# A long sequence's feed-forward by seven block products for eight (Strassen-Winograd)

## The chip, the cores and the metric

One core of one Trainium2 chip runs one launch: one layer of an encoder over two request groups. The metric is the device time of the launch in microseconds, the median of the runs. The kernel before takes 2230.62 us (three runs, 2229.17 to 2234.43).

A core has the engines PE (matrix products into PSUM, with weight loads that the profile calls PEld), DVE (vector), ACT (scalar functions and copies), POOL (GpSimd), and SP, which here issues nearly all DMAs, in order. Each works through its own list of instructions and waits for the others at semaphores.

## The reference

For each group, n tokens of 1024 features (1024 prompt tokens or 512 sample tokens, each behind 16 meta tokens that are dropped at the end) pass one mixer and one gated feed-forward. What the change touches is the last part:

```python
def conv_glu_sublayer(x, g_ffn, w_ff_gate, w_ff_up, conv_w, conv_b, w_ff_down):
    n = rms_norm(x, g_ffn)
    gate = n @ w_ff_gate
    pad = jnp.pad(gate, ((0, 0), (1, 1), (0, 0)))
    gate = pad[:, :-2] * conv_w[0] + pad[:, 1:-1] * conv_w[1] + pad[:, 2:] * conv_w[2] + conv_b
    return x + (jax.nn.gelu(gate, approximate=False) * (n @ w_ff_up)) @ w_ff_down
    ...
    h = rms_norm(h, g_final)
    return h[:, N_META:]
```

The hidden width is 2816, 22 tiles of 128. The convolution needs gate at the token before and after each one; so the first kept token needs gate of the last meta token, "column 0".

## The kernel before

Activations lie transposed, features on partitions (KT = 8 tiles of 128), tokens along the free axis. All large products are done to nearly F32 accuracy from three reduced ones: `split` (L99) makes of each operand a rounded part (hi, a cast on ACT, L102) and the remainder (lo, a subtraction, L103, on DVE or POOL), and `mm3` (L106) adds hi by hi, hi by lo and lo by hi in PSUM (L108 to L110).

The program works first through the projections and attention of both groups, with the sample group's feed-forward beside the prompt group's attention. Then `mixer_out` of the long (prompt) group, s = 0, adds the output projection to the residual h in chunks of 344, 342 and 340 tokens (`token_chunks`), squares and sums h on ACT and POOL (L486, L487) and makes each chunk's root factor `rstd` with a matmul of ones (L492) and a Newton step (L95, L96). It is merged with the rest of the sample's feed-forward.

Then PSUM is given out anew, eight tiles "mm", and `conv_glu` of s = 0 runs alone to the end of the program:

- It norms h chunk by chunk (L562, DVE) and splits it (L102; L103 on DVE and POOL by turns).
- For each of 11 pairs of tiles it forms gate in three chunks of 342 to 344 columns (two of them halo), 24 matmuls per chunk and tile, with the convolution straight out of PSUM (L585 on ACT, L586 and L588 on DVE). Gelu follows for the pair (L591). Up is formed the same way and multiplied in (L603, DVE), and the product is split.
- The pair's share of the down-projection, 8 output tiles by two chunks of 512 tokens, is formed and added to h in SBUF (L615, DVE).
- In the last pair the down-projection runs in four chunks of 256, and each is normed (L628 ff.) and stored to `yT` while the next runs; the last chunk's sum of squares is done by matmuls of ones (L656).

Weights are loaded by `load_weight` (L121) as 128 x 1024 tiles `w_f` (512 KB, SP, L125), with three buffers, in the order in which they are used, and split on ACT and DVE. Tile pools release a buffer to the next writer when its last reader is done. Nothing but the written order of the code sets the order on each engine in this part.

Of the kernel before, what the change touches and what calls it, by code (L numbers as in the profile page):

```python
# [12 lines left out]
F32 = mybir.dt.float32  # L13
# [7 lines left out]
P = 128  # L21
D = 1024
KT = D // P
NMETA = 16
HD = 64
DFF = 2816
# [57 lines left out]
def pool(ctx, g, name, bufs, side):  # L84
    return ctx.enter_context(g.tc.tile_pool(name=name, bufs=bufs, side=side, reuse_waits="tile"))
# [20 lines left out]
def mm3(g, ps, whi, wlo, xhi, xlo, start, stop):  # L106
    nc = g.nc
    nc.tensor.matmul(ps, lhsT=whi, rhs=xhi, start=start, stop=False)  # L108
    nc.tensor.matmul(ps, lhsT=whi, rhs=xlo, start=False, stop=False)  # L109
    nc.tensor.matmul(ps, lhsT=wlo, rhs=xhi, start=False, stop=stop)  # L110


def dense(g, ps, w, xhi, xlo, c0, cw, order=range(KT)):

    whi, wlo = w
    for i, k in enumerate(order):
        mm3(g, ps, whi[:, k * P:(k + 1) * P], wlo[:, k * P:(k + 1) * P],
            xhi[k][:, c0:c0 + cw], xlo[k][:, c0:c0 + cw], i == 0, i == KT - 1)
# [359 lines left out]
def add_square(g, tp, acc, h, j, c0, cw, eng, bufs=2):  # L478

    nc = g.nc  # L480
    hs = h[:, j, c0:c0 + cw]
    if j == 0:
        nc.scalar.activation(acc, hs, AF.Square)
    else:
        sq = tp.tile([P, cw], F32, name="sq", tag="sq", bufs=bufs)
        nc.scalar.activation(sq, hs, AF.Square)  # L486
        eng.tensor_tensor(out=acc, in0=acc, in1=sq, op=ALU.add)  # L487
# [5 lines left out]
    rsqrt_newton(g, tp, out, ps, cw)  # L493


def mixer_out(g, s, st, side, wp, wb, whole, tag):

    nc, tc = g.nc, g.tc
    C = SEQS[s] + 2
    h, rstd = st.h, st.rstd  # L500
    chunks = token_chunks(s)
    cm = max(w for _, w in chunks)
    with ExitStack() as es:
        mp = pool(es, g, f"fm{s}", 3, side)
        waiting = []

        def finish():
            while waiting:
                c0, cw, acc = waiting.pop(0)
                mean_rsqrt(g, mp, rstd[:, c0:c0 + cw], acc, cw, tag)  # L510

        for group in ([chunks] if whole else [[c] for c in chunks]):
            if whole:
                (xhi, xlo), base = [[x[:, k] for k in range(KT)] for x in st.x], 0
            else:
                xhi = [mp.tile([P, cm], F32R, name="xhi", tag=f"xhi{k}", bufs=2 if k >= K2 else 1) for k in range(KT)]
# [28 lines left out]
            waiting += [(c0, cw, acc[:, c0 - base:c0 - base + cw]) for c0, cw in group]  # L545
        finish()

# [116 lines left out]
        yield 4 * cw  # L664


def merge(a, wa, b, wb):
# [12 lines left out]
def drain(gen):  # L680
    for _ in gen:
        pass
# [4 lines left out]
ML = 2  # L687
K2 = 8
MB = 5
R1, R2, R3 = (1.0, 0.9), (1.0, 0.4), (1.0, 1.0)  # L690


@with_exitstack
def trunk_kernel(ctx, tc, g):
# [5 lines left out]
    for s, N in enumerate(SEQS):  # L700
# [4 lines left out]
        g.vt.append(dram.tile([5, 96, 2 * P], F32, name=f"vt{s}"))  # L705
        g.oT.append(dram.tile([D, N + 1], F32, name=f"oT{s}"))

    nc.scalar.preload_act_table_set(EXP_LN)
    g.vec = const.tile([P, V_N], F32, name="vec")
    nc.sync.dma_start(out=g.vec, in_=g.vec_in)  # L710
# [44 lines left out]
    with ExitStack() as es0:  # L755
# [4 lines left out]
    with ExitStack() as es1:  # L760
        wp = pool(es1, g, "fw1", 2, "left")
        st1 = state(es1, 1, "left", True)

        def sample():
            yield from mixer_out(g, 1, st1, "left", wp, 3, True, "mm")
            yield from conv_glu(es1, g, 1, st1, "left", wp, 3, 1)
        f1 = sample()
        with ExitStack() as es0:
            merge(attention(es0, g, 0, "right"), R2[0], f1, R2[1])
        wp0 = pool(ctx, g, "fw0", 2, "right")  # L770
        st0 = state(ctx, 0, "right", False)
        merge(mixer_out(g, 0, st0, "right", wp0, 3, False, "s"), R3[0], f1, R3[1])
        drain(f1)
    xp = pool(ctx, g, "fx0", 1, "left")
    st0.x = [xp.tile([P, KT, SEQS[0] + 2], F32R, name=nm) for nm in ("xhi", "xlo")]
    g.psum.es.close()
    g.psum = Psum(tc, "psb", mm=8)
    drain(conv_glu(ctx, g, 0, st0, "left", wp0, 3, 2))
    g.psum.es.close()


# [59 lines left out]
```

## Time and profile before

| what | value |
|---|---|
| median of three runs | 2230.62 us (2229.17 to 2234.43) |
| profiled execution | 2230.43 us |
| its span, first to last instruction | 2228.6 us |
| mean granted PE clock | 0.980 |
| long mixer_out's last matmul | starts 1460.29 us |
| first matmul of the long feed-forward | starts 1465.48 us |
| last sum of squares | starts 2216.55 us |

The profile lists, for one execution, the busy time of each engine, the chain of work that ended last, groups of like instructions, DMA issues and, from the trace, single instructions with their start (us from the span's start) and duration. PE's records overlap, since matmuls are pipelined: what one matmul costs is seen from the distance between two starts, not from its duration. A group's row gives the busy time in us, the mean of one in ns, and what ended the idle time of the engine before it.

### The profile page before, as it was taken

To read this page: it belongs to the slowest core of one execution; us is meant where nothing else is said; L and a number is where in the kernel's file an instruction comes from. 1 tells how busy PE (TensorE), PEld (TensorE's weight loads), DVE (VectorE), ACT (ScalarE), POOL (GpSimd) and SP (SyncE) were. 2 spreads that over 40 slices of the span, in tenths; PEclk is the share of its full clock that TensorE was granted. 3 is DMA by queue.
4 is the path that set the end of the run, shared out by engine and by line. 5 is a ranking of instruction groups with operands and counts; after the bars stand their busy time and mean duration, and the time that the engine had idled before them with its cause. 6 is when DMAs were issued, how large, how long until landed. Compare 5 with 4: busy or idle time off the path is not lost.

```text
span 2228.6 us, 36288 instructions
## 1 busy us (share of the span) xinstructions
PE 2128.2 (95%) x13474; PEld 1984.5 (89%) x13474; DVE 1463.7 (66%) x3453; ACT 1069.8 (48%) x1921; POOL 812.3 (36%) x649
## 2 busy tenths in 40 slices
PE   7999998997999999999999999999999999999997
PEld 6888888996987998898988899989999999999997
DVE  6876787767788777788878865784443344433446
ACT  6534566544567566776776655551222221212224
POOL 3465546864445333355444423431111000111005
PEclk9999999998999999999999999999999999999999
DMA  6555335446321322232322125721111111111112
GB/s 226 163 168 191 113 93 157 166 170 196 101 80 54 101 72 65 72 124 80 121 90 76 65 73 172 221 93 48 48 38 57 48 48 48 48 38 57 48 39 76
DMA packets 113137, 219.80 MB, mean 99 GB/s; under 512 B 13728, under 2 KB 69824, under 8 KB 112448
## 3 DMA queue, kind: packets, MB, share of 16 engines
q1 hardware_dynamic: 112960, 217.48, 30.4%
q8 instruction: 106, 1.74, 0.3%
q14 instruction: 71, 0.58, 0.1%
HBM read 168.93 MB, written 48.50 MB: 98 GB/s over the span
## 4 chain that ended last, share of the span: by engine, by line
PE 76%; DVE 12%; issue 4%; ACT 4%; DMA 3%; POOL 2%; SPq 1%; DVEq 0%; ACTq 0%; POOLq 0%
PE ps_mm L108 18%; PE ps_mm L109 18%; PE ps_mm L110 18%; PE ps_t L370 5%; PE ps_s L347 3%; PE ps_s L348 3%; DVE p L349 2%; DVE w_lo L103 2%; PE ps_o L385 1%; PE ps_o L384 1%; PE ps_s L108 1%; PE ps_s L110 1%; PE ps_s L109 1%; DMA w_f<-w_in 1%; DMA x<-xT 1%
## 5 line engine op out<-in xcount | busy, mean ns | idle before, releaser
L108 PE MATMUL ps_mm<-xhi,w_hi 128*128 128x342 f32 (+6 forms) x2320 | 726.5, 314 | 12.4 <-ACT xhi L177 6.4
L109 PE MATMUL ps_mm<-xlo,w_hi 128*128 128x342 f32 (+6 forms) x2320 | 721.3, 311 | 8.8 <-DVE xlo L103 4.6
L110 PE MATMUL ps_mm<-xhi,w_lo 128*128 128x342 f32 (+6 forms) x2320 | 719.8, 310 | 0.0
L108 PEld LDWEIGHTS ps_mm<-xhi,w_hi 128*128 128x128 f32 x2320 | 441.5, 190 | 20.2 <-ACT xhi L177 7.2
L109 PEld LDWEIGHTS ps_mm<-xlo,w_hi 128*128 128x128 f32 x2320 | 441.6, 190 | 16.3 <-DVE xlo L103 6.8
L110 PEld LDWEIGHTS ps_mm<-xhi,w_lo 128*128 128x128 f32 x2320 | 442.1, 191 | 1.0
L102 ACT CAST w_hi<-w_f 128x1024 fp32r<-128x1024 f32 x200 | 207.5, 1047 | 388.9 <-PE ps_mm L109 341.9
L103 POOL TENSOR_TENSOR a_lo<-gate,a_hi 128x256 fp32r<-128x256 f32 (+2 forms) x110 | 120.4, 1097 | 725.6 <-ACT a_hi L102 725.6
L103 DVE TENSOR_TENSOR w_lo<-w_f,w_hi 128x1024 fp32r<-128x1024 f32 x183 | 264.6, 1453 | 125.9 <-ACT w_hi L102 123.8
L349 DVE TENSOR_SCALAR_CACHE_REDUCE p<-ps_s 114x344 f32<-114x344 f32 (+4 forms) x562 | 257.6, 487 | 41.8 <-PE ps_s L348 23.3
L615 DVE TENSOR_TENSOR h<-ps_mm,h 128x512 f32<-128x512 f32 (+1 forms) x288 | 182.0, 644 | 122.3 <-PE ps_mm L110 121.4
L354 ACT ACTIVATE p<-p,nm 114x1040 f32<-114x1040 f32 (+5 forms) x212 | 215.0, 1014 | 87.3 <-DVE nm L352 84.5
L102 ACT CAST pt_hi<-ps_t 128x512 fp32r<-128x512 f32 (+6 forms) x360 | 168.8, 483 | 154.4 <-PE ps_t L370 132.4
L421 POOL TENSOR_TENSOR p<-p,r 128x1040 f32<-128x1040 f32 (+1 forms) x96 | 159.2, 1666 | 188.0 <-DVE r L356 125.7
L109 PE MATMUL ps_mm<-a_lo,w_hi 128*128 128x512 f32 (+1 forms) x576 | 216.1, 375 | 2.1 <-POOL a_lo L103 2.1
L108 PE MATMUL ps_mm<-a_hi,w_hi 128*128 128x512 f32 (+1 forms) x576 | 213.8, 382 | 2.4 <-DVE h L615 1.6
L110 PE MATMUL ps_mm<-a_hi,w_lo 128*128 128x512 f32 (+1 forms) x576 | 215.7, 374 | 0.0
L103 DVE TENSOR_TENSOR pt_lo<-ps_t,pt_hi 128x512 fp32r<-128x512 f32 (+4 forms) x312 | 171.7, 561 | 50.5 <-ACT pt_hi L102 49.0
L347 PE MATMUL ps_s<-k,q 128*114 128x348 f32 (+4 forms) x552 | 184.3, 338 | 14.3 <-DVE p L349 13.7
L370 PE MATMUL ps_t<-ident,p 128*128 128x128 f32 (+7 forms) x1188 | 183.6, 270 | 2.4 <-DVE pt_lo L103 2.1
L348 PE MATMUL ps_s<-k,q 128*114 128x348 f32 (+4 forms) x552 | 172.8, 318 | 1.3 <-DMA q<-qk 1.3
L370 PEld LDWEIGHTS ps_t<-ident,p 128*128 128x128 f32 (+7 forms) x1188 | 140.9, 136 | 31.6 <-issue 6.8
(158 smaller groups left out, 3638.3 us busy)
## 6 DMA issues: line engine op xcount, KB each, us to landing
w_f<-w_gate SPq DMA_DIRECT2D x44, 512.0 KB, 3.5
w_f<-w_up SPq DMA_DIRECT2D x44, 512.0 KB, 3.5
w_f<-w_down SPq DMA_DIRECT2D x44, 512.0 KB, 3.6
w_f<-w_in SPq DMA_DIRECT2D x36, 512.0 KB, 4.1
w_f<-w_out SPq DMA_DIRECT2D x32, 512.0 KB, 3.6
q<-qk SPq DMA_DIRECT2D x32, 257.0 KB, 3.7
q<-qk SPq DMA_DIRECT2D x48, 171.0 KB, 2.9
qk<-hi SPq DMA_DIRECT2D x42, 192.0 KB, 2.0
```

The costliest lines, as they stand in the source:

```text
L102: nc.scalar.copy(hi, src)
L103: (lo_engine or nc.vector).tensor_tensor(out=lo, in0=src, in1=hi.bitcast(F32), op=ALU.subtract)
L108: nc.tensor.matmul(ps, lhsT=whi, rhs=xhi, start=start, stop=False)
L109: nc.tensor.matmul(ps, lhsT=whi, rhs=xlo, start=False, stop=False)
L110: nc.tensor.matmul(ps, lhsT=wlo, rhs=xhi, start=False, stop=stop)
L347: nc.tensor.matmul(ps, lhsT=q[0], rhs=k[:, c0:c0 + cw], start=True, stop=False)
L348: nc.tensor.matmul(ps, lhsT=q[1], rhs=k[:, c0:c0 + cw], start=False, stop=True)
L349: nc.vector.tensor_scalar(out=p[:, c0:c0 + cw], in0=ps, scalar1=HD ** -0.5, scalar2=-3.0e38, op0=ALU.mult, op1=ALU.max, accum_out=mx[:, i: ...
L354: nc.scalar.activation(p, p, AF.Exp, bias=nm, accum_out=l)
L370: nc.tensor.transpose(tps[:, c:c + M], p[:, k0:k0 + kw], g.ident[:M, :M])
L421: nc.gpsimd.tensor_tensor(out=p, in0=p, in1=r.broadcast_to([P, n]), op=ALU.mult)
L615: nc.vector.tensor_tensor(out=hs, in0=ps, in1=hs, op=ALU.add)
```

## The change

The feed-forward of the long sequence is done by blocks of two by two, in the form of Winograd: seven products of blocks for eight, at the price of sums and differences of blocks. A block of the weights is half of a tile's 1024 columns (128 x 512); a block of the inputs is 4 feature tiles by 512 tokens.

**Inputs.** `combine_first` norms x11 and x21 (first 512 tokens) and splits them, within mixer_out's third chunk; it also keeps column 0's input, `x0`. `combine` then norms the other half, in place in h, and makes and splits t1, t2, t3, x22 and t4. Operations alternate between DVE and POOL (L739 differences, L105 remainders). Since h is overwritten, mixer_out stores h to DRAM (`g.h`).

**Gate and up.** For each pair of tiles one call of `winograd` makes gate for both tiles and both token halves, another makes up: 7 products of 12 matmuls with 512 columns. POOL makes the weights' sums s1 to s4. Gate is gathered in SBUF, 1 + 1024 columns for each tile; column 0 comes from 8 matmuls per tile with plain F32 operands of two columns (L824). Convolution, gelu and the product with up now work from SBUF. Seven combined blocks of the pair's activations are stored to DRAM (`g.act`).

**Down.** Outside the pairs' loop, product by product: q = 0 to 5 over 512 columns and q = 6 in two halves of 256, each over 11 pairs with 12 matmuls of 4 output tiles. Weights are loaded as half tiles and stay in SBUF; activations are loaded from `g.act` (L966, four buffers) and split. The residual comes back from `g.h`. The final norm of the second token half runs within q = 6, that of the first half behind its own sums.

```diff
@@ mixer_out
-                w = load_weight(g, wp, g.w_out[j], bufs=wb)
+                w = load_weight(g, wp, g.w_out[j], bufs=wb) if s == 1 else load_halves(g, wp, g.w_out[j])
...
+                    if s == 0:
+                        nc.sync.dma_start(out=g.h[j, :, c0:c0 + cw], in_=h[:, j, c0:c0 + cw])
...
+                elif j > ML and late and group[0] == chunks[-1]:
+                    for _ in range(2):
+                        next(late, None)
...
+def combine(g, st, xp, x):
...
+    def minus(out, a, b, i):
+        (nc.vector if i % 2 else nc.gpsimd).tensor_tensor(out=out, in0=a, in1=b, op=ALU.subtract)
+        return out
...
+    for i in range(HT):
+        normed(g, st, i, 1 + H)
+        kept(g, x, "t1", i, minus(x11[i], x12[i], x11[i], i))
+    for i in range(HT):
+        normed(g, st, HT + i, 1 + H)
+        kept(g, x, "t2", i, minus(x11[i], x22[i], x11[i], i))
+    for i in range(HT):
+        kept(g, x, "t3", i, minus(x12[i], x22[i], x12[i], i))
+    for i in range(HT):
+        kept(g, x, "x22", i, x22[i])
+    for i in range(HT):
+        kept(g, x, "t4", i, minus(x21[i], x21[i], x11[i], i))
...
+def winograd(g, wp, up, x, raw):
...
+    def s_(op, a, b):
+        t = up.tile([P, H], F32, name="w_s", tag="w_s", bufs=SB)
+        nc.gpsimd.tensor_tensor(out=t, in0=a, in1=b, op=op)
+        return t
...
+    s1 = s_(ALU.add, a21, a22)
+    p1 = product(split_half(g, wp, a11), x["x11"])
+    u = tile("u")
+    nc.scalar.copy(u, p1)
+    yield 0, 0, product(split_half(g, wp, a12), x["x21"]), u
+    p5 = product(split_half(g, wp, s1), x["t1"])
+    v = tile("v")
+    nc.scalar.copy(v, p5)
+    s2 = s_(ALU.subtract, s1, a11)
+    p6 = product(split_half(g, wp, s2), x["t2"])
+    add(nc.vector, u, p6, u)
+    add(nc.gpsimd, v, u, v)
+    s3 = s_(ALU.subtract, a11, a21)
+    p7 = product(split_half(g, wp, s3), x["t3"])
+    add(nc.vector, u, p7, u)
+    yield 1, 1, p7, v
+    s4 = s_(ALU.subtract, a12, s2)
+    yield 0, 1, product(split_half(g, wp, s4), x["x22"]), v
+    yield 1, 0, product(split_half(g, wp, a22), x["t4"]), u
...
+                ps = g.psum.tile(P, 2, "mm")
+                for k in range(KT):
+                    nc.tensor.matmul(ps, lhsT=raw[i][:, k * P:(k + 1) * P], rhs=g.x0[:, k],
+                                     start=k == 0, stop=k == KT - 1)
...
+            nc.vector.tensor_tensor(out=t, in0=ps, in1=rest, op=ALU.add)
+            nc.gpsimd.tensor_tensor(out=a, in0=t, in1=a, op=ALU.mult)
...
+        kept_act("x11", x11)
+        kept_act("x21", x21)
+        kept_act("x22", x22)
+        t2 = minus("t2", x22, minus("t1", x12, x11))
+        minus("t3", x22, x12)
+        minus("t4", x21, t2)
...
+    for q, (c0, cw) in [(q, (0, H)) for q in range(6)] + [(6, (0, H // 2)), (6, (H // 2, H // 2))]:
+        ps = [g.psum.tile(P, cw, "mm") for _ in range(HT)]
+        for f in range(NP):
+            w = operand(q, f)
+            if f == 0 and q < 2:
+                a = xs[:, q * H:(q + 1) * H]
+            else:
+                a = op.tile([P, H], F32, name="a_f", tag="a_f", bufs=AF_)[:, :cw]
+                nc.sync.dma_start(out=a, in_=g.act[f, q, :, c0:c0 + cw])
+            ahi, alo = (t[:, :cw] for t in split_act(g, wp, a, cw))
+            w = split_half(g, wp, w)
+            for j in range(HT):
+                mm3(g, ps[j], *block(w, j), ahi, alo, f == 0, f == NP - 1)
```

In the diff, H = 512, HT = 4, the weight halves have five buffers (`w_hi`, `w_lo`), the sums `w_s` two, and `split_half` splits with ACT and DVE. The lines below are what stands on three engines; each row has the line, the operation, its output and inputs and their shape, and xN for N alike in a row. Line numbers are those of the changed kernel where its rows are shown.

On POOL, at the start of the long feed-forward, there stood before only the remainders of the normed chunks (`xlo`) and then those of the first activations (`a_lo`):

```order
L487 TENSOR_TENSOR acc<-acc,sq 128x340
L103 TENSOR_TENSOR xlo<-t,xhi 128x344 x4
L103 TENSOR_TENSOR xlo<-t,xhi 128x342 x4
L103 TENSOR_TENSOR xlo<-t,xhi 128x340 x4
L103 TENSOR_TENSOR a_lo<-gate,a_hi 128x342 x2
```

In the changed kernel, at the same place, the end of the combined inputs (`h` for the differences, `t_lo` and `x_lo` for the remainders; eleven such rows stand ahead) and then the first sums of weights (`w_s`):

```order
L105 TENSOR_TENSOR t_lo<-h,t_hi 128x512
L739 TENSOR_TENSOR h<-h 128x512
L105 TENSOR_TENSOR t_lo<-h,t_hi 128x512 x4
L739 TENSOR_TENSOR h<-h 128x512 x2
L767 TENSOR_TENSOR w_s<-w_f 128x512
L767 TENSOR_TENSOR w_s<-w_s,w_f 128x512
L767 TENSOR_TENSOR w_s<-w_f 128x512
L767 TENSOR_TENSOR w_s<-w_f,w_s 128x512
L767 TENSOR_TENSOR w_s<-w_f 128x512
L780 TENSOR_TENSOR v<-u,v 128x512
```

So s1, which the third product reads, comes behind all of them.

On SP, the queue of the loads, before had whole weight tiles only, in the order of their use:

```order
L125 DMA w_f<-w_down 128x1024 x2
L125 DMA w_f<-w_gate 128x1024 x2
L125 DMA w_f<-w_up 128x1024 x2
L125 DMA w_f<-w_down 128x1024 x2
L644 DMA yT<-y 128x2x256 x16
```

In the changed kernel, from the last store of a difference (`act_101<-a_t`) to the first loads of activations for the down-projection (`a_f`); a name such as a_6 is a half tile of w_down for pair 6:

```order
L850 DMA act_101<-a_t 128x512
L885 DMA a_7_23054<-w_down 128x512
L885 DMA a_8_23078<-w_down 128x512
L885 DMA a_8_23080<-w_down 128x512
L885 DMA a_9_23104<-w_down 128x512
L885 DMA a_10_23128<-w_down 128x512
L885 DMA a_10_23130<-w_down 128x512
L885 DMA a_1_23182<-w_down 128x512
L885 DMA a_1_23184<-w_down 128x512
L885 DMA a_2_23208<-w_down 128x512
L885 DMA a_3_23232<-w_down 128x512
L966 DMA a_f<-act_101 128x512 x4
```

The loads of activations now stand behind a store that waits for POOL, and behind weight loads of later pairs.

On PE, at the first products of gate, the changed kernel has behind the last chunk's sum (`ps_s<-acc,ones_d`) matmuls of 512 columns and among them the two-column ones for column 0 (`x_18861` is `x0`):

```order
L520 MATMUL ps_s<-acc,ones_d 128x340
L110 MATMUL ps_mm<-x_hi,w_hi 128x512 x2
L824 MATMUL ps_mm<-x_18861,w_f 128x2 x8
L111 MATMUL ps_mm<-x_lo,w_hi 128x512
L112 MATMUL ps_mm<-x_hi,w_lo 128x512
L110 MATMUL ps_mm<-x_hi,w_hi 128x512
```

The matmuls of chunks with 344 columns, which stood there before, are gone.

More of the change, by code (lines that the diff above doesn't have):

```diff
@@ L23 @@
 KT = D // P
+H = D // 2
+HT = KT // 2
 NMETA = 16
@@ L113, in dense, with block, split_half, load_whole @@
 def dense(g, ps, w, xhi, xlo, c0, cw, order=range(KT)):
+    for i, k in enumerate(order):
+        mm3(g, ps, *block(w, k), xhi[k][:, c0:c0 + cw], xlo[k][:, c0:c0 + cw], i == 0, i == KT - 1)
+def block(w, k):
     whi, wlo = w
[L116 to L118 removed]
+    if isinstance(whi, list):
+        whi, wlo, k = whi[k // 4], wlo[k // 4], k % 4
+    return whi[:, k * P:(k + 1) * P], wlo[:, k * P:(k + 1) * P]
+def split_half(g, wp, src, lo_engine=None):
+    hi = wp.tile([P, H], F32R, name="w_hi", tag="w_hi", bufs=HB)
+    lo = wp.tile([P, H], F32R, name="w_lo", tag="w_lo", bufs=HB)
+    split(g, hi, lo, src, lo_engine)
+    return hi, lo
+def load_whole(g, wp, src):
+    w = wp.tile([P, D], F32, name="w_f", tag="w_f", bufs=WB)
+    g.nc.sync.dma_start(out=w, in_=src)
+    return w
+def load_halves(g, wp, src):
+    w = load_whole(g, wp, src)
+    parts = [split_half(g, wp, w[:, i * H:(i + 1) * H]) for i in range(2)]
+    return [p[0] for p in parts], [p[1] for p in parts]
 def load_weight(g, wp, src, bufs=2, ahead=2, lo_engine=None):
@@ L664, in conv_glu, with normed, kept, inputs @@
         yield 4 * cw
+def normed(g, st, k, c0):
+    hs = st.h[:, k, c0:c0 + H]
+    g.nc.vector.scalar_tensor_tensor(out=hs, in0=hs, scalar=g.gain[:, V_GFFN + k:V_GFFN + k + 1],
+                                     in1=st.rstd[:, c0:c0 + H], op0=ALU.mult, op1=ALU.mult)
+    return hs
+def kept(g, x, nm, i, src):
+    split(g, x[nm][0][:, i], x[nm][1][:, i], src, g.nc.gpsimd if i % 2 else g.nc.vector)
+def inputs(pl, names):
+    return {nm: [pl.tile([P, HT, H], F32R, name=f"{nm}_{part}") for part in ("hi", "lo")] for nm in names}
@@ new lines, in combine_first @@
+def combine_first(g, st, xp, x):
+    nc = g.nc
+    x.update(inputs(xp, ("x11", "x21")))
+    g.x0 = xp.tile([P, KT, 2], F32, name="x0")
+    for i in range(2):
+        nc.vector.scalar_tensor_tensor(out=g.x0[:, :, i], in0=st.h[:, :, 0], scalar=st.rstd[:, 0:1],
+                                       in1=g.gain[:, V_GFFN:V_GFFN + KT], op0=ALU.mult, op1=ALU.mult)
+    for nm, k0 in (("x11", 0), ("x21", HT)):
+        for i in range(HT):
+            kept(g, x, nm, i, normed(g, st, k0 + i, 1))
+            yield
@@ L689 @@
 MB = 5
+HB = 5
+WB = 3
+SB = 2
+AT = 3
+AF_ = 4
+LAGF = 5
+TS = ("x11", "x21", "t2", "t1", "t3", "x22", "t4")
 R1, R2, R3 = (1.0, 0.9), (1.0, 0.4), (1.0, 1.0)
```

215 lines of the change are left out of this document (199 added, 16 removed).

## The prediction

> **What bounds the kernel now.** First the head of the page and its chain of work, shares of the span by engine.
> ```profile
> span 2228.6 us, 36288 instructions
> PE 2128.2 (95%) x13474; PEld 1984.5 (89%) x13474; DVE 1463.7 (66%) x3453; ACT 1069.8 (48%) x1921; POOL 812.3 (36%) x649
> PE 76%; DVE 12%; issue 4%; ACT 4%; DMA 3%; POOL 2%; SPq 1%; DVEq 0%; ACTq 0%; POOLq 0%
> ```
> The sum below is made against this execution: span 2228.6, time 2230.43, so 1.8 us lie around the span; the median of the runs, 2230.62, is the same within 0.2 us. An average over the program says little about the changed stage, so next the table of windows (us from the start; busy time of PE, PEld, DVE, ACT, POOL; granted clock, DMA share, GB/s).
> ```profile
> 1360.00:1460.00 100.00, 100.00 (x648) 99.50 (x647) 68.08 (x117) 53.58 (x98) 38.65 (x35) 0.99 0.69 214
> 1460.00:1480.00 20.00, 14.96 (x69) 12.35 (x69) 18.27 (x27) 9.62 (x20) 8.46 (x9) 0.83 0.24 82
> 1500.00:1600.00 100.00, 100.00 (x562) 93.22 (x561) 43.24 (x64) 20.91 (x28) 13.97 (x12) 1.00 0.16 52
> 2000.00:2100.00 100.00, 100.00 (x580) 94.93 (x579) 42.87 (x62) 22.11 (x29) 6.86 (x6) 1.00 0.14 48
> ```
> In the long feed-forward (about 1466 to 2217) PE is full, DVE 43%, ACT some 22%, POOL 7 to 14%, DMA 15%. Only PE sets the time there, and the others have room for additions. The one hole is its start, 1460 to 1480. The chain of work by time gives the period of a pair of tiles: the same matmul comes back every 67.14 us.
> ```profile
> 1582.86 0.24 PE ps_mm L108
> 1650.00 0.24 PE ps_mm L108
> 1717.14 0.24 PE ps_mm L108
> ```
>
> **Removed and added on PE.** Overlapping records hide a matmul's cost; the step between the starts of weight loads (PEld), or of matmuls, shows it.
> ```profile
> 1500.01 0.19 PEld L109 LDWEIGHTS ps_mm<-xlo,w_hi 128*128 128x128 f32 x1
> 1502.83 0.19 PEld L109 LDWEIGHTS ps_mm<-xlo,w_hi 128*128 128x128 f32 x1
> 1535.09 0.19 PEld L108 LDWEIGHTS ps_mm<-a_hi,w_hi 128*128 128x128 f32 x1
> 1536.90 0.19 PEld L110 LDWEIGHTS ps_mm<-a_hi,w_lo 128*128 128x128 f32 x1
> 2203.87 0.28 PE L110 MATMUL ps_mm<-a_hi,w_lo 128*128 128x256 f32 x1
> 2205.66 0.28 PE L110 MATMUL ps_mm<-a_hi,w_lo 128*128 128x256 f32 x1
> ```
> Some 342 columns: 18 steps in 2.82 us, 0.157 each. 512 columns: 8 steps in 1.81, 0.226. 256 columns: 15 steps in 1.79, 0.119. Before, a pair has 288 x 0.157 + 96 x 0.226 = 66.9 us, the measured period. After, gate and up have 2 x 84 matmuls of 512 columns: 168 x 0.226 = 38.0.
>
> New beside them are 16 plain F32 matmuls of two columns per pair (line 824 of the change), for gate's column 0. An F32 matmul leaves two records, as the profile's eight calls of L656 show, so 32 records per pair, 352 in all. Nothing like them is in the trace; these rows bound them.
> ```profile
> L656 PEld LDWEIGHTS ps_mm<-sq,ones_d x16: 186/190/192, 2208.1 to 2218.3; 128*128 128x128 f32 x16
> 1332.83 0.57 PEld L370 LDWEIGHTS ps_t<-ident,p 114*128 114x128 f32 x5
> 2216.55 2.32 PE L656 MATMUL ps_mm<-sq,ones_d 128*128 128x256 f32 x10
> ```
> Loads back to back in the second row come (0.57 - 0.19)/4 = 0.095 apart; a whole load alone takes 0.19. I take 0.10, by the row with narrow work that follows itself, and keep 0.19: 3.2 us per pair (to 6.1). Gate and up: 41.2 x 11 = 453 us, of which the first pair's p1, p2 and column 0 (7 us) run before the hole, so 446 to 447 behind it.
>
> Down: q0 to q5 are 6 x 11 x 12 = 792 matmuls, 179.0; q6's two halves 264 x 0.119 = 31.4; the sums of squares are one F32 matmul of 512 columns and, ahead of the last sum, one half's five of 256; by the last row above a record of 256 takes 2.32/10, less its tail 0.215: 4 x 0.215 + 10 x 0.215 = 3. Together 213.5, say 214.
>
> **The start.** These rows show the sum for the last chunk, its rstd, and DVE and POOL beside each other.
> ```profile
> 1464.68 1.50 PE L492 MATMUL ps_s<-acc,ones_d 128*128 128x340 f32 x2 [4.07 <-POOL acc L487]
> 1470.48 0.50 DVE L96 SCALAR_TENSOR_TENSOR rstd<-rstd,rs_y 128x340 f32<-128x340 f32 x1
> 1466.77 1.06 DVE L562 SCALAR_TENSOR_TENSOR t<-h,gain,rstd 128x344 f32<-128x344 f32 x2
> 1473.53 1.63 DVE L562 SCALAR_TENSOR_TENSOR t<-h,gain,rstd 128x342 f32<-128x342 f32 x2
> 1473.51 0.79 POOL L103 TENSOR_TENSOR xlo<-t,xhi 128x344 fp32r<-128x344 f32 x1 [1.45 <-ACT xhi L102]
> 1459.09 1.21 DVE L103 TENSOR_TENSOR w_lo<-w_f,w_hi 128x1024 fp32r<-128x1024 f32 x1
> 1463.78 1.92 DVE L103 TENSOR_TENSOR w_lo<-w_f,w_hi 128x1024 fp32r<-128x1024 f32 x1
> 1464.58 1.77 POOL L103 TENSOR_TENSOR xlo<-t,xhi 128x344 fp32r<-128x344 f32 x1
> ```
> Before, PE could start on chunk 1 at 1465.5, while the other chunks were being normed. After, gate's p5 needs s1 (line 767), which stands on POOL behind 18 combining operations (lines 105 and 739); these need the last chunk's rstd, 1471, and DVE's norming. At 0.79 x 512/344 = 1.18, say 1.25 us each, they are 22.5 us from about 1479; with s1, its cast and its remainder, 2.1, p5 starts at 1504. That is the lower end. The upper comes from the overlap: two t on DVE take 1.06 with POOL idle and 1.63 beside a POOL operation of 0.79, and the w_lo of 1.21 takes 1.92 beside one. So either engine delays the other by most of its operation; if fully, DVE's some 22 operations of 0.6 to 0.7 us add 13 to 15 us: 1517. I take 1511. mixer_out's h stores, 4.2 MB beside 214 GB/s at share 0.69, stay hidden, at worst 2 us.
>
> By the Trainium skill, page "SBUF — State Buffer", section "🔬 SBUF: two separate sides", a DVE operation with two SBUF inputs and a GpSimd operation that reads SBUF exclude each other for the whole instruction. The 1.63 beside 1.06 agrees; by that rule alone p5 would start at 1517, without it at 1504.
>
> After an idle of 4.07 us the clock was 0.83 in that window; I add 2 us for its recovery after each of the two long idles. Gate and up end at E = 1511 + 447 + 2 = 1960.
>
> **Gate and up, steadily.** Per pair POOL has 18 operations, 22.5 of 41.2 us. DVE has 14 half remainders at 0.61, 12 sums out of PSUM at 0.69 and 4 conv steps of 1024 at three times the 0.53 of a t: 23 us. ACT has 14 half casts at 0.53, copies, conv and gelu: some 15. The rows:
> ```profile
> L615 DVE TENSOR_TENSOR h<-ps_mm,h 128x512 f32<-128x512 f32 x240 | 162.6, 689 | 111.6 <-PE ps_mm L110 110.8
> L102 ACT CAST w_hi<-w_f 128x1024 fp32r<-128x1024 f32 x200 | 207.5, 1047 | 388.9 <-PE ps_mm L109 341.9 <-PE ps_s L109 20.1 <-DMA w_f<-w_in 12.1
> L103 POOL TENSOR_TENSOR a_lo<-gate,a_hi 128x342 fp32r<-128x342 f32 x44 | 40.6, 924 | 556.8 <-ACT a_hi L102 556.8
> L103 POOL TENSOR_TENSOR a_lo<-gate,a_hi 128x340 fp32r<-128x340 f32 x22 | 34.4, 1565 | 64.7 <-ACT a_hi L102 64.7
> ```
> The tightest place is the turn of a pair: the next gate's s2 stands on POOL behind up's last product (line 846) and differences (line 854). From that product's end: sum on DVE 0.7, four POOL operations 4.9, cast and remainder 1.3: 6.9 us, under p1, p2, column 0 and p5 on PE, 3 x 2.7 + 1.6 = 9.7. I cost it at nothing. The last row's 1565 ns would be 2.36 at 512 columns: then 0.7 + 9.4 + 1.3 = 11.4, a stall of 1.7 per pair.
>
> **Turn to down.** On SP the act loads of q0's f = 1 to 4 (line 966) stand behind the last act stores and some ten weight loads of 256 KB.
> ```profile
> w_f<-w_gate SPq DMA_DIRECT2D x44, 512.0 KB, 3.5
> 2.00:25.00 23.00, 17.81 (x97) 16.18 (x98) 12.59 (x22) 16.75 (x27) 0.00 (x0) 1.00 1.01 355
> ```
> The last store waits for POOL's last difference, E + 5.5. Ten loads at about 340 GB/s are 7.5 us, the landing some 3: f = 1 starts at E + 16.4, where f = 0 ended at E + 2.7. PE idles 13.7, and about 4 more at f = 5, behind 16 further loads. So 18, from 12 (POOL and loads overlapping) to 30 (1.16 us a load, at the 1360 window's 214 to 226 GB/s); with the clock 20. q0 and q1 need 245 GB/s (28 blocks of 0.262 MB in 30 us), under that row's 355; later products read weights that lie in SBUF, and POOL's sums run ahead. A product fills four of eight PSUM tiles, so its four copies of 0.69 on DVE lie under the next product. Before, SP had only whole loads in the order of use, and nothing waited.
>
> **Sum.** 1960 + 20 + 214 = 2194 for the start of the last sum; from 2216.55 to the end of the span before are 12 us, kept, as the last half is normed alike. Span 2206, time **2208**, 1.0% under 2230.4. Of 755 us between holes PE saves some 73 (67.1 - 60.6 a pair), and some 50 of it goes to the start and the turn.
>
> **Rivals.**
> - *The start and turn cost less.* p5 at 1504 (-7), turn 12 (-6): 2195; with records of 0.09, 2191. For it: POOL's 0.79 beside DVE's t is as short as any, so POOL may win the overlap, and loads may flow while the last differences are still computed. Against: POOL's 1.77, and the store that blocks SP. 0.17.
> - *Slower: the narrow records cost whole loads.* At 0.19, 352 x 0.09 = +32: 2240. It decides from 0.163 on (22.4/352 more than 0.10). For it: F32 loads of L656 take 190 ns each. Against: loads of 190 ns do follow each other at 0.119. 0.10.
> - *POOL becomes the bound.* 1.7 x 10 at the turns, or 18 x 2.36 = 42.5 against 41.2 a pair, and 1517 at the start: 2208 + 17 + 6 = 2231, or 2225 without the start's part. For it, 1565 ns in a stage with DVE at 43%; against, 924 ns in the same stage. 0.10. The skill's rule above gives POOL and DVE together 22.5 + 14.5 = 37 of 41.2 us in the steady stage, which still fits.
> - *The turn runs at the lower DMA rate*, 30: 2220. 0.08.
> - *The change isn't effective*: PE would not run products alone, or stalls in every product for an input: over 2240. 0.03.
>
> **Chances.** The forecast has 0.52. About 0.2% (4.5 us: under 2226, over 2235) is what a measurement of this kernel can tell from no change. Faster takes the forecast, the first and fourth rivals and a part of the third, 0.80; same 0.07; slower 0.13. The range reaches to the second rival and the first: 2190 to 2238.
>
> **What would show it.** In the changed profile: a period of 41.2 us per pair, with records of line 824 about 0.10 apart; PE full between two holes; the first ending at p5 near 1511 with POOL as releaser, the second some 14 us long ending with DMA a_f; products of 30 us in down. A period over 43 us, a PE wait for w_s at each turn, or holes in q0 and q1 for a_f would make the prediction wrong.

## The result and the profile after

The changed kernel takes 2250.44 us (median of four runs, 2247.06 to 2252.82), before 2231.43 on the same chip: a ratio of 1.0083, 95% interval 1.0065 to 1.0101. It is slower by 0.8%, where 1.0% faster was forecast, and outside the stated range. The profiled execution's span is 2248.7 us, where the sum of the prediction gave 2206: 42.7 us are to be explained.

The head of its page, with the chain of work:
```profile
PE 2082.4 (93%) x12410; PEld 1848.9 (82%) x12410; DVE 1656.9 (74%) x3555; ACT 1185.6 (53%) x2156; POOL 1157.3 (51%) x849
PE 68%; DVE 13%; DMA 5%; issue 5%; ACT 4%; POOL 4%; SPq 1%; POOLq 0%; DVEq 0%; ACTq 0%
```
PE's busy time fell by only 46 us, DVE's rose by 193 and POOL's by 345, and DMA's share of the chain went from 3% to 5%. The table of windows (columns as before: PE, PEld, DVE, ACT, POOL, clock, DMA share, GB/s) tells the stages apart:
```profile
1500.00:1520.00 20.00, 4.86 (x11) 3.63 (x12) 12.03 (x11) 6.53 (x12) 17.78 (x13) 0.50 0.00 1
1700.00:1800.00 100.00, 100.00 (x472) 82.34 (x472) 64.59 (x72) 38.35 (x57) 60.06 (x41) 1.00 0.26 91
1980.00:2000.00 20.00, 3.37 (x15) 2.42 (x13) 0.69 (x1) 0.00 (x0) 8.73 (x7) 0.70 0.97 340
2020.00:2060.00 40.00, 36.96 (x149) 26.66 (x148) 40.00 (x26) 17.36 (x29) 38.77 (x24) 1.00 0.25 75
2200.00:2248.00 48.00, 34.66 (x254) 32.23 (x254) 37.32 (x71) 26.09 (x58) 9.70 (x7) 0.92 0.40 131
```
Gate and up keep PE full (1700 to 1800). The two holes are there (start, turn). What was not foreseen: at 2020 to 2060, in the second half of q0 and the first of q1 in down, DVE and POOL are both busy nearly all the time and PE is not full, and PE's share is low again in q6, from 2194 on.

PE's two long waits; what their releaser, a cast on ACT, had itself waited for (s1 on POOL, the first sum of weights; the load of f = 1's activations); the period of a pair (column 0's matmuls in the chain); and the steps in gate and up (34 loads) and in down (six matmuls):
```profile
1515.14 0.79 PE L110 MATMUL ps_mm<-t_hi,w_hi 128*128 128x512 f32 x1 [22.70 <-ACT w_hi L104]
2001.58 2.08 PE L110 MATMUL ps_mm<-w_hi 128*128 128x512 f32 x4 [18.21 <-ACT w_hi L104]
```
```profile
1512.12 1.71 POOL L767 TENSOR_TENSOR w_s<-w_f 128x512 f32<-128x512 f32 x1
2000.39 0.62 ACT L104 CAST w_hi<-a_f 128x512 fp32r<-128x512 f32 x1 [27.71 <-DMA a_f<-act]
```
```profile
1531.83 1.68 PE ps_mm L824 x16
1574.57 1.68 PE ps_mm L824 x16
```
```profile
1566.01 0.19 PEld L111 LDWEIGHTS ps_mm<-t_lo,w_hi 128*128 128x128 f32 x1
1573.94 0.19 PEld L112 LDWEIGHTS ps_mm<-t_hi,w_lo 128*128 128x128 f32 x1
```
```profile
2131.37 0.39 PE L110 MATMUL ps_mm<-w_hi 128*128 128x512 f32 x1
2132.73 0.39 PE L110 MATMUL ps_mm<-w_hi 128*128 128x512 f32 x1
```
A pair takes 42.74 us, not 41.2. The sixteen records of column 0 take 1.68 us, 0.105 each, as forecast. But a matmul of 512 columns takes 0.2332 in gate and up (7.93/34), and 0.2267 in down (1.36/6).

The stretch in down, on DVE (remainders), POOL (sums of weights, line 889) and PE, one after the other:
```profile
2050.66 1.78 DVE L105 TENSOR_TENSOR w_lo<-a_f,w_hi 128x512 fp32r<-128x512 f32 x1
2052.36 1.77 DVE L105 TENSOR_TENSOR w_lo<-a,w_hi 128x512 fp32r<-128x512 f32 x1
2054.05 1.78 DVE L105 TENSOR_TENSOR w_lo<-a_f,w_hi 128x512 fp32r<-128x512 f32 x1
...
2064.22 0.68 DVE L105 TENSOR_TENSOR w_lo<-a_f,w_hi 128x512 fp32r<-128x512 f32 x1
```
```profile
2050.15 1.74 POOL L889 TENSOR_TENSOR a<-w_s,a 128x512 f32<-128x512 f32 x1
2051.85 1.73 POOL L889 TENSOR_TENSOR a<-a,a 128x512 f32<-128x512 f32 x1
```
```profile
2052.49 0.50 PE L111 MATMUL ps_mm<-w_lo,w_hi 128*128 128x512 f32 x1 [0.27 <-DVE w_lo L105]
2055.89 0.50 PE L111 MATMUL ps_mm<-w_lo,w_hi 128*128 128x512 f32 x1 [0.28 <-DVE w_lo L105]
```
Both engines issue every 1.70 us and each record lasts 1.7 to 1.8, though the last DVE row shows that the same remainder takes 0.68 when it starts while POOL is idle. They take turns. A step f of down needs two remainders, so it lasts 2 x 1.70 = 3.40 us, and PE, which needs 2.72, waits for the remainder at each step. The same pattern comes back in q5, where POOL adds the residual and the squares:
```profile
2172.10 1.74 POOL L924 TENSOR_TENSOR v<-v,res 128x512 f32<-128x512 f32 x1
2172.61 1.78 DVE L105 TENSOR_TENSOR w_lo<-a_f,w_hi 128x512 fp32r<-128x512 f32 x1
```

### The profile page after: what moved, and what is told of

Same layout as the page of the kernel before. It is cut to its first block, busy times and chain, and to the rows that moved or that the text cites. A ratio compares the mean times of both kernels' runs of the same rounds, so it can differ in the third digit from the quotient of the medians.

```text
span 2248.7 us, 35598 instructions
## 1 busy us (share of the span) xinstructions
PE 2082.4 (93%) x12410; PEld 1848.9 (82%) x12410; DVE 1656.9 (74%) x3555; ACT 1185.6 (53%) x2156; POOL 1157.3 (51%) x849
## 4 chain that ended last, share of the span: by engine, by line
PE 68%; DVE 13%; DMA 5%; issue 5%; ACT 4%; POOL 4%; SPq 1%; POOLq 0%; DVEq 0%; ACTq 0%
PE ps_mm L110 15%; PE ps_mm L111 15%; PE ps_mm L112 15%; DVE w_lo L105 5%; PE ps_t L398 5%; PE ps_s L375 3%; PE ps_s L376 3%; DVE p L377 2%; DMA w_f<-w_in 2%; PE ps_mm L824 2%; PE ps_o L413 1%; PE ps_o L412 1%; PE ps_s L110 1%; PE ps_s L112 1%; PE ps_s L111 1%
## 5 line engine op out<-in xcount | busy, mean ns | idle before, releaser
L110 PE MATMUL ps_mm<-xhi,w_hi 128*128 128x258 f32 (+3 forms) x1264 | 388.9, 308 | 12.9 <-ACT xhi L205 6.9
L111 PE MATMUL ps_mm<-xlo,w_hi 128*128 128x258 f32 (+3 forms) x1264 | 381.8, 302 | 8.5 <-DVE xlo L105 4.3
L112 PE MATMUL ps_mm<-xhi,w_lo 128*128 128x258 f32 (+3 forms) x1264 | 380.2, 301 | 0.0
L105 DVE TENSOR_TENSOR w_lo<-w_f,w_hi 128x512 fp32r<-128x512 f32 (+1 forms) x215 | 262.6, 1227 | 84.8 <-ACT w_hi L104 84.0
L104 ACT CAST w_hi<-w_f 128x512 fp32r<-128x512 f32 (+1 forms) x232 | 188.5, 820 | 145.6 <-PE ps_mm L111 86.2
L110 PEld LDWEIGHTS ps_mm<-xhi,w_hi 128*128 128x128 f32 x1264 | 241.6, 191 | 19.8 <-ACT xhi L205 7.8
L111 PEld LDWEIGHTS ps_mm<-xlo,w_hi 128*128 128x128 f32 x1264 | 241.6, 191 | 13.6 <-DVE xlo L105 5.4
L112 PEld LDWEIGHTS ps_mm<-xhi,w_lo 128*128 128x128 f32 x1264 | 241.1, 191 | 1.0
L105 DVE TENSOR_TENSOR pt_lo<-ps_t,pt_hi 128x512 fp32r<-128x512 f32 (+4 forms) x312 | 171.8, 562 | 49.0 <-ACT pt_hi L104 47.7
L110 PE MATMUL ps_s<-xhi,w_hi 128*128 128x256 f32 (+4 forms) x480 | 148.2, 312 | 9.7 <-ACT xhi L205 7.2
L112 PE MATMUL ps_s<-xhi,w_lo 128*128 128x256 f32 (+4 forms) x480 | 147.2, 307 | 6.6 <-DVE w_lo L105 6.4
```

The lines of the kernel that those rows point to most:

```text
L104: nc.scalar.copy(hi, src)
L105: (lo_engine or nc.vector).tensor_tensor(out=lo, in0=src, in1=hi.bitcast(F32), op=ALU.subtract)
```

## The experiments

The part ahead of the change moves by up to 10 us from run to run (p5 of the first pair starts between 1509 and 1519 where its stage is as in the changed kernel). So a single run is read by stages: from p5's first matmul to the first matmul of down (E), and from there to the last sum of squares. A stage that an edit leaves alone differs by under 1 us between the runs of this table. In us:

| kernel | p5 | E | last sum | span | gate and up | down |
|---|---|---|---|---|---|---|
| changed | 1515.14 | 1980.44 | 2235.95 | 2248.7 | 465.3 | 255.5 |
| sums_on_dve | 1509.15 | 1973.99 | 2221.50 | 2234.3 | 464.8 | 247.5 |
| acts_early | 1509.44 | 1975.12 | 2217.52 | 2230.3 | 465.7 | 242.4 |
| x_aligned | 1512.28 | 1967.17 | 2222.34 | 2235.1 | 454.9 | 255.2 |
| mended | 1513.62 | 1968.85 | 2198.81 | 2211.6 | 455.2 | 230.0 |

The prediction had 449 for gate and up (447 and 2 for the clock) and 234 for down, the turn included. Down by products, from the first matmul of one to that of the next (q6: to the last sum), with what PE alone needs by its steps of 0.2267, and for q6 the prediction's 31.4 + 3:

| kernel | q0 | q1 | q2 | q3 | q4 | q5 | q6 |
|---|---|---|---|---|---|---|---|
| PE alone | 29.9 | 29.9 | 29.9 | 29.9 | 29.9 | 29.9 | 34.4 |
| changed | 56.6 | 33.9 | 30.6 | 29.9 | 29.9 | 32.8 | 41.9 |
| sums_on_dve | 53.1 | 29.9 | 29.9 | 29.9 | 29.9 | 33.0 | 41.8 |
| acts_early | 34.5 | 36.5 | 37.2 | 29.9 | 29.9 | 32.7 | 41.8 |
| mended | 34.7 | 30.3 | 30.4 | 29.9 | 29.9 | 32.9 | 41.8 |

### Down: DVE and POOL taking turns

**sums_on_dve.**
```diff
     def sum_(out, op_, a, b):
-        nc.gpsimd.tensor_tensor(out=out, in0=a, in1=b, op=op_)
+        nc.vector.tensor_tensor(out=out, in0=a, in1=b, op=op_)
```


> Down's sums of weights (q2 to q4) are done by DVE in place of POOL. Theory: in q1 to q3 POOL's sums and DVE's remainders exclude each other, so that each step f lasts 2 x (1.09 + 0.61) = 3.40 us where PE needs 2.72. With the sums on DVE, two remainders and two sums are 4 x 0.61 = 2.4 us, below 2.72: the steps in this stretch come to 2.72, and the end moves up by 8 to 12 us against the changed kernel. Rival: the inputs come late from DRAM or from ACT; then the steps stay near 3.4, or get longer by the work that DVE has more.

Measured: 2236.47 us against 2250.44; down 247.5 for 255.5, so 8 us of the 14 are the edit's and 6 came from ahead of it. The sums run in q0 and q1, earlier than the expectation had them; there the steps are 2.72 us from q0's f = 6 on. The same window (down starts 6.5 us earlier here), and DVE within it:
```profile
2020.00:2060.00 40.00, 40.00 (x178) 33.12 (x177) 33.96 (x55) 20.41 (x35) 2.73 (x2) 1.00 0.32 98
```
```profile
2032.75 0.68 DVE L105 TENSOR_TENSOR w_lo<-a,w_hi 128x512 fp32r<-128x512 f32 x1
2033.35 0.68 DVE L889 TENSOR_TENSOR a<-a,a 128x512 f32<-128x512 f32 x1
2033.96 0.68 DVE L105 TENSOR_TENSOR w_lo<-a_f,w_hi 128x512 fp32r<-128x512 f32 x1
```
DVE does 55 operations in 40 us where it did 26, and PE is full: more work on DVE, less wait. The inputs were not late; the theory holds, at the lower end of its size. q5 stays at 33.0: what POOL does there is not among the sums that were moved.

### The turn

**acts_on_act_queue.**
```diff
-                nc.sync.dma_start(out=a, in_=g.act[f, q, :, c0:c0 + cw])
+                (nc.scalar if q == 0 and f < 5 else nc.sync).dma_start(out=a, in_=g.act[f, q, :, c0:c0 + cw])
```


> The first four loads of activations of q0 in down go out from ACT's queue and not from SP's. Theory: the 18.2 us hole at the turn is the place of these loads on SP, behind the last act stores and some twenty weight loads; from ACT's queue they can land some 5 us after the last product's start, f = 1 starts when its weights are there, some 8 to 10 us earlier, and the second wait (at f = 5) may grow by a few us. Rival: the weights themselves land no earlier (5.4 us each, under load), and the hole stays within 3 us of 18.

Measured: 2249.17 us, a hole of 18.39. The rival's size, and a miss for the theory. The trace shows why the queue did not matter (ACT's issues, then the chain of waits):
```profile
1993.71 4.35 ACTq L966 DMA_DIRECT2D a_f<-act  x4
```
```profile
1984.79 5.54 DMA a<-w_down
1990.33 0.02 issue
1990.35 5.34 DMA a<-w_down
1995.69 0.02 issue
1995.70 5.90 DMA a<-w_down
```
ACT, idle since 1971, issued them only at 1993.7: the trace has eight semaphores that the loads use in turn, and each load waits for the one eight places ahead of it in the program's order, whichever engine issues it (the first of the four went out at 1993.71, as the half weight issued at 1988.06 had landed at 1993.69). So the half weights follow each other in rounds of some 5.4 us while the DMA engines run at a share near 1 (0.97 and 340 GB/s at 1980 to 2000 in the changed kernel).

**acts_early.** The activations of pairs 1 to 6 get tiles of their own and are loaded during gate and up.
```diff
+    ep = pool(ctx, g, "fe0", 1, "right")
+    first_acts = {}
...
+        if f0 + 2 == NFF:
+            for f in range(1, 7):
+                first_acts[f] = ep.tile([P, H], F32, name=f"act_{f}")
+                nc.sync.dma_start(out=first_acts[f], in_=g.act[f, 0])
...
+            elif q == 0 and f in first_acts:
+                a = first_acts[f]
```


> The activations that q0 of down reads for f = 1 to 6 are loaded during gate and up into tiles of their own, as soon as they are stored. Theory, after the run in which they only changed queues: at the turn the loads of some twenty half weights fill the DMA engines (384 GB/s at a share of 1.04), and an activation load that stands behind them lands late on whichever queue. With these activations in SBUF ahead of the turn, f = 1 waits for its own weights alone: the hole of 18.2 us falls below 7, the second wait at f = 5 goes, and the end moves up by 10 to 16 us. Rival: the weights of f = 1 land no earlier than 18 us after f = 0 (DMA rate alone, whatever the order); the hole stays above 14.

Measured: 2232.05 us, down 242.4 for 255.5. The hole is gone:
```profile
1986.58 0.50 PE L111 MATMUL ps_mm<-w_lo,w_hi 128*128 128x512 f32 x1 [0.15 <-DVE w_lo L105]
1997.11 2.07 PE L110 MATMUL ps_mm<-w_hi 128*128 128x512 f32 x4 [2.29 <-ACT w_hi L104]
```
```profile
1980.00:2000.00 20.00, 17.55 (x71) 13.80 (x70) 12.73 (x14) 6.95 (x12) 5.90 (x4) 0.92 1.04 380
2020.00:2060.00 40.00, 35.28 (x137) 23.83 (x137) 40.00 (x28) 14.70 (x24) 40.00 (x25) 1.00 0.26 77
```
The weights of f = 1 were there in time; what PE waited for was the activation behind the other weights. The gain of 13.1 us is less than the hole, since the stretch with DVE and POOL by turns (second row) now costs more: PE 35.3 of 40 us where it had 37.0, and q1 and q2 take 36.5 and 37.2 us where they had 33.9 and 30.6.

### The start

**sums_first.** The first gate pair's s1 to s4 are written ahead of `combine`.
```diff
+    raw0 = [load_whole(g, wp, g.w_gate[i]) for i in range(2)]
+    b11, b12, b21, b22 = (w[:, i * H:(i + 1) * H] for w in raw0 for i in range(2))
+    early = [xp.tile([P, H], F32, name=f"s{i}_first") for i in range(4)]
+    for out, op_, a, b in ((early[0], ALU.add, b21, b22), (early[1], ALU.subtract, early[0], b11),
+                           (early[2], ALU.subtract, b11, b21), (early[3], ALU.subtract, b12, early[1])):
+        nc.gpsimd.tensor_tensor(out=out, in0=a, in1=b, op=op_)
+    combine(g, st, xp, x)
...
```


> The four sums of weights of the first gate pair are made on POOL ahead of the combined inputs. Theory: the hole at the start (PE idle to 1515) is POOL's eighteen combining operations, behind which the sums stood; with the sums ahead, p5 to p7 follow t1, t2, t3 as these get ready, p5 at about 1493 to 1500, and the first pair ends some 8 to 12 us earlier. Rival: DVE and POOL together are the bound, so that the four sums moved ahead only push the combined inputs back by their 4 x 1.3 to 1.7 us; then the first pair ends within 4 us of where it did, and the hole is spread over several smaller ones.

Measured: 2248.96 us. p5 starts at 1500.84, but waits follow:
```profile
1500.84 0.50 PE L110 MATMUL ps_mm<-t_hi,w_hi 128*128 128x512 f32 x1 [1.13 <-ACT t_hi L104]
1506.38 0.79 PE L111 MATMUL ps_mm<-t_lo,w_hi 128*128 128x512 f32 x1 [5.05 <-DVE t_lo L105]
1518.24 1.22 PE L110 MATMUL ps_mm<-t_hi,w_hi 128*128 128x512 f32 x2 [6.86 <-ACT t_hi L104]
```
From the last chunk's sum in mixer_out to the second column-0 block of the first pair it is 60.7 us (1470.42 to 1531.13), in the changed kernel 65.1 (1466.71 to 1531.83). 4.4 us are gained, near the rival's bound of 4 (the other runs, with the start as it was, lie within 1 us of 65.1): POOL's order sets where the hole lies, DVE and POOL together how long it is. In the changed kernel POOL's first difference shows how they exclude each other:
```profile
1482.09 6.48 POOL L739 TENSOR_TENSOR h<-h 128x512 f32<-128x512 f32 x1 [2.83 <-DVE x_lo L105]
1488.53 1.09 POOL L105 TENSOR_TENSOR x_lo<-h,x_hi 128x512 fp32r<-128x512 f32 x1
```
It lasts 6.48 us, while DVE does a run of remainders and differences back to back; a remainder on POOL lasts 1.09 in the next row.

### The step of a matmul in gate and up

**x_layout.**
```diff
+    gap = {"t1": 256, "t2": 2 * H, "t3": 16}
...
+        if nm == "x21":
+            both = pl.tile([P, HT, 2, H], F32R, name="x21_both")
+            out[nm] = [both[:, :, 0], both[:, :, 1]]
...
+            hi = pl.tile([P, HT * H + gap.get(nm, 0)], F32R, name=f"{nm}_hi")
...
+    for i in range(HT):
+        for ps, w, b in ((p4, w4, x["x22"]), (p3, w3, x["t4"])):
+            mm3(g, ps, *block(w, i), b[0][:, i], b[1][:, i], i == 0, i == HT - 1)
...
```


> Gate and up take 0.2333 us per matmul of 512 columns in the changed kernel, where 0.226 was forecast and where its own down-projection runs at 0.2265. Here the distance in SBUF between the rounded part and the remainder of an input is 2 KB for x21, 9 KB for t1, 12 KB for t2, 8 KB + 64 B for t3 and 8 KB as it was for x11; the products with x22 and t4 are run in turn, three matmuls each, so that consecutive matmuls go to two PSUM tiles. If the place of the moving operand sets the step, products with x21, t1, t2 or t3 run at another step than x11's 0.2333. If accumulating twelve times into one PSUM tile does, only the last pair of products gets faster, towards 0.227. If neither does (the work of the other engines, or the stage as such), all stay at 0.233. The whole gains at most 12 us where one of them holds for all products.

Measured: 2247.64 us; only x22 and t4, which ran by turns, were fast: 0.2267 over 18 steps, all others 0.233.
```profile
1611.25 0.39 PE L111 MATMUL ps_mm<-t_lo,w_hi 128*128 128x512 f32 x1
1615.33 0.39 PE L111 MATMUL ps_mm<-t_lo,w_hi 128*128 128x512 f32 x1
```
I took that for the effect of two PSUM tiles; but the gaps had moved x22 and t4 as well.

**two_banks.** `products` runs two products by turns, three matmuls to one PSUM tile and three to the other.
```diff
...
+    p1, p2 = products((split_half(g, wp, a11), x["x11"]), (split_half(g, wp, a12), x["x21"]))
...
+    p5, p3 = products((split_half(g, wp, s1), x["t1"]), (split_half(g, wp, a22), x["t4"]))
...
+    p7, p4 = products((split_half(g, wp, s3), x["t3"]), (split_half(g, wp, s4), x["x22"]))
...
```


> In gate and up three of the four pairs of products (p1 with p2, p5 with p3, p7 with p4) are run in turn, three matmuls to one PSUM tile and three to the other; p6 stays alone. Theory: the step of 0.2333 us comes of twelve matmuls in a row into one PSUM tile, as the last pair of products showed when it was run in turn (0.2267). Then 144 of a pair's 168 matmuls gain 0.0066, and the period of a pair falls from 42.74 to about 41.8, 10 us in all. Rival: the step in that run came of something else in that place (the inputs x22 and t4, the moment at the end of a pair): then p1/p2 and p5/p3 stay at 0.233 and the period falls by 0.3 at most. Either way p6 follows two more products, so that no new wait for the sum s2 is expected.

Measured: 2254.11 us, and that theory falls: a pair takes 42.73 us (1529.27 to 1572.00 in the chain). The new order also lengthened the turn's hole to 32.27 us.

**three_mended** puts this order together with sums_on_dve and acts_early.

> Three edits at once: down's sums of weights on DVE, q0's activations early, products of gate and up in two PSUM tiles by turns. By the theories the savings against the changed kernel add up, since they lie in three stages one behind the other: 14 us (measured alone), 10 to 16, and about 10; together 34 to 40, so some 2212 us, about 0.9 below the time of before per hundred. Rival: the savings overlap, since a start of down that comes earlier meets the same limit of DVE later (q1 waits for its remainders all the same); then 20 to 28 us, 2222 to 2230, hardly below before.

Measured: 2238.05 us, ratio 1.0035 against before (1.0023 to 1.0047), a miss, above the theory's 2212 and the rival's 2222 to 2230: no gain in gate and up, and a wait of 16.25 us at the turn in spite of the early activations.

**x_aligned.** What x22 and t4 had in x_layout was their place, counted from the tiles in the code: 224 bytes behind a multiple of 256, like the weights' halves and, in down, the split activations.
```diff
+    xp.tile([P, 32], F32, name="pad")
     x.update(inputs(xp, ("x11", "x21")))
-    g.x0 = xp.tile([P, KT, 2], F32, name="x0")
+    g.x0 = xp.tile([P, 64], F32, name="x0")[:, :2 * KT].rearrange("p (k i) -> p k i", i=2)
```


> The inputs of gate and up start 224 bytes behind a multiple of 256 in SBUF, as the weights' halves and down's activations do (pads of 128 and 192 bytes); in the changed kernel they start 96 or 160 behind one. In the run with several layouts only x22 and t4 stood at 224, and only they ran at 0.2267; in turns of two PSUM tiles the step stayed 0.2333 where the inputs stood at 96 or 160. Theory: the place of the moving operand within 256 bytes sets the step; then all products of gate and up run at 0.2267, the period of a pair falls from 42.74 to 41.6, and the end moves up by 12 us. Rival: it was x22's and t4's place by some other measure (their distance from the weights, or taking turns together with it): the period then stays above 42.3.

Measured: 2236.87 us, gate and up 454.9 for 465.3. A pair takes 41.77 us:
```profile
1528.71 1.68 PE ps_mm L825 x16
1570.48 1.68 PE ps_mm L825 x16
```
All products run at 0.2267, and 10.4 us are gone without an instruction added or removed on PE. Two kernels ask whether it is the inputs' own place or that against the weights.

**seven_offsets.**
```diff
+    pad = {"x11": 40, "x21": 8, "t1": 56, "t2": 16, "t3": 16, "x22": 40, "t4": 32}
...
+        pl.tile([P, pad[nm]], F32, name=f"{nm}_pad")
...
```


> Each of the seven inputs of gate and up starts at another place within 256 bytes: x11 at 0, x21 at 32, t1 at 64, x22 at 96, t2 at 128, t3 at 192, t4 at 224; the weights' halves stay at 224. Theory A (the moving operand's own place): some places run at 0.2267 and the others at 0.2333, t4 among the fast; 0, a full line, would be expected fast too. Theory B (its place against the weights'): only t4 at 224 is fast, all others 0.2333. x22 at 96 is the slow place of the changed kernel.

Measured: 2249.36 us; t4's matmuls (first two rows, six steps in 1.36 us) run at 0.2267; x22 (last two, six steps in 1.40), x11, t1, t2 and t3 at 0.233; x21, at 32, at about 0.229.
```profile
1637.34 0.39 PE L112 MATMUL ps_mm<-t_hi,w_lo 128*128 128x512 f32 x1
1638.70 0.39 PE L112 MATMUL ps_mm<-t_hi,w_lo 128*128 128x512 f32 x1
```
```profile
1634.08 0.40 PE L110 MATMUL ps_mm<-x_hi,w_hi 128*128 128x512 f32 x1
1635.48 0.40 PE L110 MATMUL ps_mm<-x_hi,w_hi 128*128 128x512 f32 x1
```

**weights_at_192.** On top of x_aligned's edit:
```diff
...
+    pool(ctx, g, "fpad", 1, "right").tile([P, 8], F32, name="pad_w")
     wp0 = pool(ctx, g, "fw0", 2, "right")
```


> Inputs at 224 bytes as in the aligned run, but the weights' halves, and with them down's split activations, moved by 32 bytes to 192. Theory A (the moving operand's own place): gate and up keep 0.2267; down runs as its new place 192 does in the run with seven places. Theory B (place against the weights'): gate and up fall back to 0.2333, down stays at 0.2267, since its operands and weights moved together.

Measured: 2247.70 us. Gate and up are back at 42.77 us a pair (1529.35 to 1572.12), with the inputs where they were in x_aligned:
```profile
1560.07 0.39 PE L110 MATMUL ps_mm<-t_hi,w_hi 128*128 128x512 f32 x1
1565.66 0.39 PE L110 MATMUL ps_mm<-t_hi,w_hi 128*128 128x512 f32 x1
```
24 steps in 5.59 us, 0.233, and a step f of down stays 2.72 us. So it is the place of the moving operand against that of the weights (theory B).

### Together

**mended** is x_aligned, acts_early and sums_on_dve in one kernel.

> The three edits that act on different stages together: inputs at 224 bytes (gate and up), q0's activations loaded early (the turn), down's sums of weights on DVE (down). By the theories the savings add up: 12 + 17 (2249 to 2232, alone) + 11 to 14 (alone 14), so 2206 to 2213 us and about 0.99 of before, the time that was forecast for the change as it stood. Rival: in down the earlier start only meets DVE's limit of two remainders and two sums per step, or the alignment brings nothing; then 2218 to 2226.

Measured: 2214.75 us, median of five runs; ratio 0.9933 against before, 0.9919 to 0.9946. It is faster than both kernels, 1.7 us above the expected 2206 to 2213. Down takes 230.0 us, 25.5 less than in the changed kernel, where the two edits alone gave 8.0 and 13.1; together with gate and up's 10.1 it is 35.6. So the savings don't overlap; in down they are more than the two alone, since acts_early by itself ran into a longer stretch of DVE and POOL by turns (q1 and q2 above), which sums_on_dve takes away.

## Why the prediction was wrong

- **Bound and arithmetic of PE: right.** PE set the time in gate and up, column 0's records took 0.105 us (0.10), and p5 started at 1515 (1511, upper end 1517), its idle ended by POOL's first sum s1 and its cast. So the first hole ended 4 us later than the sum had it; 2 of these lie ahead of the change, where the last chunk's sum starts at 1466.71 and before at 1464.68, and that place moves by more than this from run to run.
- **The 512 step in gate and up: wrong, 10 us.** "168 x 0.226" took the step from the old down-projection for inputs that lie elsewhere in SBUF. At 0.2333 it is 1.1 us more per pair. x_aligned gave 10.4 us back. The rest of the 16.3 us by which gate and up were over the forecast is 5.9: a pair takes 41.77 even when aligned, 0.57 over the 41.2, of which column 0's records (3.36 for 3.2) and some 0.1 us by which the matmul behind each of their two blocks comes late are the part that the trace shows.
- **The turn: mechanism right, partly mis-sized.** PE's idle at f = 1 was forecast as 13.7 us and is 18.2; at f = 5 it was forecast as 4 and is 1.8. The term most off is the landing of a load, put at some 3 us: the activation that was issued at 1994.89 was cast at 2000.39, 5.5 later. With PE's slow clock behind the hole (0.87 at 2000 to 2020) the stage took some 22 us for its 20. That the loads' place in SP's queue was the cause was wrong in one point: their place among the DMAs counts, not the queue (acts_on_act_queue 0, acts_early 13).
- **Down: this step failed.** "[...] later products read weights that lie in SBUF, and POOL's sums run ahead" costed down behind the turn at PE's 214 us alone. That POOL ran ahead is just what hurt. The prediction had the exclusion, with rows (1.63 beside 1.06 us), and weighed it for gate and up, where 37 of 41.2 us still fit; in down, where each 2.72 us need two remainders, it wasn't weighed. Steps of 3.40 us where 2.72 was priced, in the second half of q0, six of q1's, one of q2's and four of q5's, cost some 12 us more than PE's time up to q6; sums_on_dve gave 8 back. Its own sign, products of 30 us in down, failed in q1 (33.9) and q5 (32.8). The rule of the Trainium skill that the prediction named (page "SBUF — State Buffer", section "🔬 SBUF: two separate sides") agrees: both engines' records fill 1.7 us and alternate.
- **q6: left out, some 7 us.** From 2194.08 to 2235.95 it took 41.9 us for the 34.4 of the sum. About 3 of it lie between 2196 and 2203, beside POOL's four sums of squares (6.12 us from 2195.36 on), where DVE's remainders of 512 columns take 1.7 to 1.8 us again; most of the rest comes beside the norm of the second half, which is on DVE among the remainders (37.3 of 48 us in the last window). No run changed q6, nor q5's 3 us: the causes there are read from the trace alone.

The sum: 4 (start), 16 (gate and up), 2 (turn), 12 (down to q6), 7.5 (q6) and under 1 for the tail make the 42.7. By its time alone the last rival came true (over 2240, chance 0.03), but not by its mechanism: PE runs the products, and is full in gate and up, q3 and q4. The rival nearest in mechanism, POOL as the bound at 2231, had the right pair of engines in the wrong stage. Whole loads for narrow records were excluded by 0.105. A side count, 73 us saved on PE, is 71.5 by its own 6.5 us a pair; the time was not made from it.

In mended gate and up take 455.2 us (449 forecast) and down 230.0 (234), so the time comes near the forecast of 2208, but in part by luck. The early activations take out a hole that the forecast had priced at 20, and 16 us above PE's 214 are left in down: 5 in q0, 1 in q1 and q2, 3 in q5 and 7 in q6. The forecast was nearly what the idea is worth, but not what this code was worth.

## What to carry to other kernels

Fewer products for more sums pays only where the engines that make the sums have time in every stage, the shortest step of the busiest stage first: write down, per PE step, each other engine's operations there, and add DVE's with two SBUF inputs to POOL's, since they take turns. Before a load is moved to another queue, see whether the DMA engines are full and which earlier loads it waits for; here another queue gave nothing, and loading earlier gave 13 us. When matmuls of one size differ in step between stages, compare the addresses of their operands before looking for a busy engine.

## What the runs showed of the hardware

- A matmul of 512 columns of the three-part product takes 0.2267 us where the moving operand and the weights start at the same place modulo 256 bytes in SBUF, and 0.2333 where they differ by 32, 96 or 128 bytes, or by 64 with the inputs below (seven_offsets, weights_at_192, the changed kernel). With the inputs 64 above (x21) it was about 0.229, but t4, too, needed some six matmuls behind a slow product to reach 0.2267, so twelve are too few to tell. Moving either side changes it. What in the chip does this is open.
- DVE and POOL, with two SBUF inputs each, alternate for some 45 us in down, 1.70 us for one operation of each at 512 columns (DVE's alone start 0.60 apart in sums_on_dve, so some 1.1 of it is POOL's). Turns are not assured: at the start a POOL operation lasted 6.48 us while DVE did a run of them back to back.
